# A hybrid mixer layer on one core: the RWKV mixer in three parts, squares on ScalarE, operands placed anew

## The chip, the cores and the metric

The kernel runs on one core of one Trainium2 chip. A core has a matrix engine (TensorE, PE below; its weight loads are listed apart as PEld), a vector engine (VectorE, DVE), a scalar engine (ScalarE, ACT), a general engine (GpSimd, POOL), queues that issue DMAs (SyncE, SP), an on-chip memory with 128 partitions (SBUF) and accumulator banks (PSUM). The metric is device time in microseconds of one execution. Before the change its median was 1709.05 us over three runs (1708.21 to 1712.27).

## The reference

One layer over x of 256 tokens by 2048 features, all in float32. Cut to what is computed:

```
h = rms_norm(x, norm_mix_pre)
z = h @ w_in                          # 2048 x 14800: parts of four mixers and four gates of 2048
o_conv = short_conv_mixer(z_conv)     # gated causal convolution over 3 tokens
o_gla  = gla_mixer(z_gla)             # gated linear attention, chunks of 64 tokens
o_diff = diff_attention_mixer(z_diff) # two softmax maps, their difference
o_rwkv = rwkv7_mixer(z_rwkv)          # state += (state . -kk) b + v k, token by token
merged = sum over n of sigmoid(z_gate[n]) * (o_n @ w_branch[n])
x = x + rms_norm(merged @ w_out, norm_mix_post)
h = rms_norm(x, norm_ffn_pre)
out = x + rms_norm((silu(h @ w_gate) * (h @ w_up)) @ w_down, norm_ffn_post)
```

## The kernel before

Every product of float32 matrices is made of three products of float32r: an operand is split into a rounded part "hi" and the exact remainder "lo", and hi·hi, hi·lo and lo·hi are summed in PSUM. Weights stream from DRAM in chunks of 256 rows by 512 columns (`Stream.chunk`, from L574): SP loads `raw`, ACT casts it to `hi` (L585), DVE subtracts to get `lo` (L586). `raw` has four buffers, `hi` and `lo` three each, and the chunk's instructions have a raised priority, so that the scheduler puts them ahead of other work of their engine.

There are two kinds of products with the normalised input, which lies feature-major as `hT_hi` and `hT_lo`. `gemm_feat` (L666 to L668) gives features by tokens: the weight slice is stationary and 256 tokens move through. `gemm_tok` (L646 to L648) gives tokens by features: a slice of hT (or of a mixer's output oT, of the merged mT, of h2) is stationary and 512 weight columns move through. The down projection has the same form in L1024 to L1026, with the activations `ah` and `al` stationary. The first projection (called L: 464 columns, tiles of 112, 96, 128 and 128) runs while x is still being loaded; `x_piece` makes hT_hi on ACT (L351) and hT_lo on DVE (L352) piece by piece. `x_norm` sums the squares of x (L705, L707, L709, all on POOL) for the factor of each token, which is multiplied in behind the products; its `pow` is L715.

Then come three projections rk, rr and rv, the RWKV mixer, three projections c1, c2 and c0 of the convolution, the convolution's four gate projections of 96 matmuls each with 24 matmuls of w_branch behind each (`gates_and_branch`: the sigmoid on ACT, the product with it on DVE in L764), then gqk, two gv projections and gated linear attention, the RWKV mixer's gates, differential attention, the remaining gates, w_out, and the feed-forward part.

PE takes instructions in the order in which the scheduler put them. It places the mixer's instructions among the projections that follow it by priority: `e.mix` (100000) for the mixer, `e.boost` (200000) for the weight chunks, 2·e.boost for the steps of the mixer's four chunks. The mixer's last stretch before those steps inverts 32 triangular 64 x 64 blocks. POOL inverts their 32 x 32 halves in 31 steps (L244, L246). DVE copies a transposed half (L248), POOL writes it and the halves to DRAM and reads them back (L251 to L263), and PE joins the halves by two products (L268, L272), each drained by DVE (L269, L273). After the chunk steps the outputs are transposed (L330), scaled by DVE (L338), passed twice through POOL (L340, L341) and split by ACT (L342) and DVE (L343). All the mixer's tiles are in a pool R, which is closed before the convolution is written down; the pool S1 of gated linear attention takes the same room later. PSUM has four banks "mm" for the projections, two "ps" and two "psl".

Where the operands lie, in bytes within a partition: hi at 36000 + 4096·b, lo at 48288 + 4096·b, hT_hi at 60576, hT_lo at 76960, all at 160 modulo 512. oT and mT lie at 480, ah and al at 224 modulo 512. The slices that L takes as stationary begin at 160, 96, 480 and 480.

Of the kernel before, what the change touches and what calls it, by code (L numbers as in the profile page):

```python
# [75 lines left out]
def rwkv_mixer(e, Zr, Zk, Zv, Zl, wa, g2, out_hi, out_lo):  # L76
    """Z*: [128, 4, 257] feature-major projections with a zero column in front."""
# [18 lines left out]
    # token shift  # L96
# [15 lines left out]
    # decay, in-context rate, gate  # L112
# [19 lines left out]
    C = m4("C")  # L132
# [11 lines left out]
    # normalised key direction  # L144
# [22 lines left out]
    # k' = k (1 + (a - 1) k_a)  # L167
# [7 lines left out]
    # bonus  # L175
# [8 lines left out]
    # scaled operands, [b | k] and [a | r] side by side within a chunk  # L184
# [12 lines left out]
    # value, token-major, under the rows of sa  # L197
# [14 lines left out]
    # intra-chunk products, transposed: rows [b s | k s], columns [a t | r t]  # L212
# [17 lines left out]
    # N = (I - U)^-1 of the 32 strictly upper 64 x 64 blocks U = AM[b rows, a columns]  # L230
# [17 lines left out]
    V.tensor_copy(NT[0:32], NN[0:32].rearrange("p a b -> p b a"))  # L248
# [9 lines left out]
    for hf in range(2):  # L258
        ms = slice(16 * hf, 16 * hf + 16)
# [4 lines left out]
        Zt = m4("Zt", (32, 16, 32))  # L264
        ps = e.ps()
# [8 lines left out]
    # chunks  # L274
# [4 lines left out]
    for c in range(4):  # L279
# [8 lines left out]
        X = e.M.tile([128, 8, 64], F32, tag="X", name="X", bufs=2)  # rows of sa; of the output  # L288
# [23 lines left out]
        # group norm per head  # L312
# [79 lines left out]
def gla_mixer(e, q, k, wl, v, g, wa2, out_hi, out_lo):  # L392
    """q (scaled), k: [128, 2, 256] feature-major; wl: [16, 256]; v, g: [128, 2, 512] token-major."""
# [15 lines left out]
    # log(1 + x) = 2 atanh(x / (2 + x))  # L409
# [13 lines left out]
    # scores, transposed [s, t]: within a tile of 128 [hh, i, j], and from tile 0 to tile 1 [hh, j]  # L423
# [3 lines left out]
    # the diagonal: q . k of each token and head  # L427
# [12 lines left out]
    # pairs whose halves of a block of 2w differ, scaled about the middle of the block  # L440
# [59 lines left out]
def diff_mixer(e, q, k, v, lq, out_hi, out_lo):  # L500
    """q (scaled), k: [128 (map, d), 4 heads, 256] feature-major; v: [128, 2, 512]; lq: [128, 4, 64]."""
# [3 lines left out]
    lp = e.T_.tile([128, 2, 64], F32, tag="lp", name="lp")  # L505
# [45 lines left out]
def conv_mixer(e, cu, b, rB, y, out_hi, out_lo):  # L551
    """cu: [128, 4, 258] (C * u behind two zero columns), b: two banks [128, 2, 256], rB [128, 256] their factor; y: [128, 4, 256] scratch."""
# [15 lines left out]
# blocks of 512 columns of w_in as chunks() of it holds them  # L568
# [3 lines left out]
class Stream:  # L572
    """Weights in: DMA -> (rounded part, exact remainder), both float32r."""
# [16 lines left out]
def hybrid_kernel(tc, x, xt, w_l, w_in, w_branch, w_out, w_gate, w_up, w_down, post_mix, post_ffn, wa2_d, w2_d, a2_d, g2_d, lq_d,  # L590
# [9 lines left out]
    with ExitStack() as ctx:  # L600
# [25 lines left out]
        def rms(ssum, n, eps):  # L626
            """ssum [128, 1] <- (ssum / n + eps) ** -0.5"""
# [509 lines left out]
```

## Time and profile before

| | |
|---|---|
| median of three runs | 1709.05 us |
| the profiled execution: span | 1707.7 us |
| mean granted clock of PE | 0.990 |
| busy: PE | 1665.4 us (98%), 8630 matmuls |
| busy: DVE | 987.1 us (58%) |
| busy: ACT | 753.0 us (44%) |
| busy: POOL | 190.0 us (11%) |
| DMA | 306.84 MB, mean 180 GB/s |

PE is busy nearly all the time. The chain of work that ended last is a chain of matmuls whose largest steps are L646 to L648 (9% of the span each). In a row of the timeline the number in brackets is how long the engine had been idle before the instruction, and what released it. Matmuls overlap: their recorded duration is longer than the distance from one start to the next, and it is the distance that adds up to the span. The granted clock is given as a share of full speed, 2.4 GHz; 0.50 is 1.2 GHz.

### The profile page before, as it was taken

Reading aid. Unit: us, or ns where it says so; the run is one execution under the profiler, and the core shown is the slowest. Engines: PE = TensorE matmul, PEld = TensorE weight load, DVE = VectorE, ACT = ScalarE, POOL = GpSimd, SP = SyncE. Lnnn points to the kernel's source line nnn. Section 1 sums busy time; section 2 is a strip of 40 time slices with the busy share of each in tenths; the row PEclk is TensorE's granted clock in tenths of the full one; section 3 lists DMA queues with packets and bytes.
Section 4 is the critical chain, followed back from the end, with each engine's and each line's share of the span. In section 5 each row is a group of like instructions: output and inputs, shape, how many; then the busy total and the mean of one; then the engine's idle time right before and its main releaser. Section 6 shows DMA issues by size and latency. Waiting matters only on the chain. (4 is left out here: it accounts for less than half of the span.)

```text
span 1707.7 us, 21846 instructions
## 1 busy us (share of the span) xinstructions
PE 1665.4 (98%) x8630; PEld 1402.6 (82%) x8630; DVE 987.1 (58%) x1040; ACT 753.0 (44%) x873; POOL 190.0 (11%) x168
## 2 busy tenths in 40 slices
PE   7999998999999999999999899999999999999997
PEld 6999976897788987888888788888888888888886
DVE  7667644669764458545554655445455554556555
ACT  3444342335544335544444644444444444445443
POOL 4005192111210001201000100000000000000001
PEclk8999998999999999999999999999999999999999
DMA  6654445445446554765555466565565555555653
GB/s 210 201 182 136 146 161 153 141 136 185 148 149 196 186 174 161 257 196 186 185 185 185 150 209 193 187 188 193 187 197 187 190 191 186 184 190 184 194 186 134
DMA packets 86087, 306.84 MB, mean 180 GB/s; under 512 B 9713, under 2 KB 12033, under 8 KB 85473
## 3 DMA queue, kind: packets, MB, share of 16 engines
q1 hardware_dynamic: 84208, 298.50, 54.4%
q0 software_dynamic: 1200, 5.90, 1.1%
q8 instruction: 67, 1.10, 0.3%
q10 hardware_dynamic: 576, 1.05, 0.2%
q14 instruction: 36, 0.29, 0.0%
HBM read 302.40 MB, written 3.01 MB: 179 GB/s over the span
## 5 line engine op out<-in xcount | busy, mean ns | idle before, releaser
L586 DVE TENSOR_TENSOR lo<-raw,hi 128x1024 fp32r<-128x1024 f32 (+1 forms) x556 | 699.2, 1259 | 597.3 <-ACT hi L585 596.6
L585 ACT CAST hi<-raw 128x1024 fp32r<-128x1024 f32 (+1 forms) x556 | 583.4, 1050 | 759.6 <-PE mm L648 532.4
L647 PE MATMUL mm<-lo,h_hi 128*128 128x512 f32 x704 | 275.0, 391 | 0.4 <-DVE lo L586 0.4
L648 PE MATMUL mm<-hi,h_lo 128*128 128x512 f32 x704 | 274.0, 390 | 0.0
L647 PE MATMUL mm<-lo,hT_hi 128*128 128x512 f32 x608 | 240.9, 396 | 13.3 <-DVE lo L586 13.2
L646 PE MATMUL mm<-hi,h_hi 128*128 128x512 f32 x704 | 250.2, 391 | 0.5 <-ACT h_hi L351 0.5
L648 PE MATMUL mm<-hi,hT_lo 128*128 128x512 f32 x608 | 238.9, 393 | 0.0
L646 PE MATMUL mm<-hi,hT_hi 128*128 128x512 f32 x608 | 221.7, 393 | 0.0
L668 PE MATMUL mm<-hT_hi,lo 128*128 128x256 f32 (+2 forms) x640 | 183.1, 289 | 10.3 <-DVE lo L586 10.3
L666 PE MATMUL mm<-hT_hi,hi 128*128 128x256 f32 (+1 forms) x640 | 185.2, 290 | 1.8 <-ACT hi L585 1.8
L667 PE MATMUL mm<-hT_lo,hi 128*128 128x256 f32 (+1 forms) x640 | 184.2, 289 | 0.0
L647 PEld LDWEIGHTS mm<-lo,h_hi 128*128 128x128 f32 x704 | 132.2, 188 | 28.0 <-DVE lo L586 0.9
L646 PEld LDWEIGHTS mm<-hi,h_hi 128*128 128x128 f32 x704 | 132.2, 188 | 27.8 <-ACT h_hi L351 0.7
L648 PEld LDWEIGHTS mm<-hi,h_lo 128*128 128x128 f32 x704 | 132.2, 188 | 27.0
L647 PEld LDWEIGHTS mm<-lo,hT_hi 128*128 128x128 f32 x608 | 114.8, 189 | 40.0 <-DVE lo L586 15.4
L646 PEld LDWEIGHTS mm<-hi,hT_hi 128*128 128x128 f32 x608 | 114.7, 189 | 24.4
L648 PEld LDWEIGHTS mm<-hi,hT_lo 128*128 128x128 f32 x608 | 114.8, 189 | 23.7 <-issue 0.3
L668 PEld LDWEIGHTS mm<-hT_hi,lo 128*128 128x128 f32 (+2 forms) x640 | 123.8, 194 | 11.5 <-DVE lo L586 11.2
L666 PEld LDWEIGHTS mm<-hT_hi,hi 128*128 128x128 f32 (+1 forms) x640 | 124.5, 194 | 3.2 <-ACT hi L585 2.2
L667 PEld LDWEIGHTS mm<-hT_lo,hi 128*128 128x128 f32 (+1 forms) x640 | 124.3, 194 | 1.1 <-issue 0.2
L629 POOL TENSOR_TENSOR s1f<-s1f,mhalf 128x1 f32<-128x1 f32 x2 | 1.1, 540 | 721.1 <-DVE s1f L628 721.1
L767 POOL TENSOR_TENSOR acc<-acc,gt 128x512 f32<-128x512 f32 x24 | 41.5, 1748 | 332.2 <-DVE gt L766 332.2
(351 smaller groups left out, 1892.5 us busy)
## 6 DMA issues: line engine op xcount, KB each, us to landing
raw<-in_w_in_dram SPq DMA_DIRECT2D x224, 512.0 KB, 3.5
raw<-in_w_gate_dram SPq DMA_DIRECT2D x88, 512.0 KB, 3.5
raw<-in_w_up_dram SPq DMA_DIRECT2D x88, 512.0 KB, 3.5
raw<-in_w_down_dram SPq DMA_DIRECT2D x88, 512.0 KB, 3.5
raw<-in_w_branch_dram SPq DMA_DIRECT2D x32, 512.0 KB, 3.5
raw<-in_w_out_dram SPq DMA_DIRECT2D x32, 512.0 KB, 3.5
raw<-in_w_l_dram SPq DMA_DIRECT2D x8, 464.0 KB, 5.8
xs<-in_x_dram POOLq DMA_DIRECT2D x1, 2048.0 KB, 12.9
```

The source lines that it names most:

```text
L585: nc.scalar.copy(hi[:, :, :w], raw[:, :, :w])
L586: nc.vector.tensor_tensor(lo[:, :, :w], raw[:, :, :w], hi[:, :, :w].bitcast(F32), op=ALU.subtract)
L629: G.tensor_tensor(ssum, ssum, e.mhalf.to_broadcast(list(ssum.shape)), op=ALU.pow)
L646: mm(banks[i_], ah[:, ts], hi[:, k, :], start=kt == 0, stop=False)
L647: mm(banks[i_], ah[:, ts], lo[:, k, :], start=False, stop=False)
L648: mm(banks[i_], al[:, ts], hi[:, k, :], start=False, stop=kt == nk - 1)
L666: mm(ps, hi[:, k, cs], hT_hi[:, kt, :], start=first, stop=False, skip_group_check=True)
L667: mm(ps, hi[:, k, cs], hT_lo[:, kt, :], start=False, stop=False, skip_group_check=True)
L668: mm(ps, lo[:, k, cs], hT_hi[:, kt, :], start=False, stop=last, skip_group_check=True)
L767: G.tensor_tensor(cs, cs, gt[:, i], op=ALU.add)
```

## The change

There are three edits, and each moves other things.

1. `x_norm`: the four squares go from POOL to ACT, the five additions from POOL to DVE.
2. `rwkv_mixer` is a generator in three parts. The first ends with the DMAs of the inverse; its copy L248 is POOL's now (L249 after the change). The second, the products that join the halves, is issued from the convolution's `gates_and_branch`, behind the sigmoid of the third gate (g = 2), and uses the two PSUM banks which that gate has just left. The third, the chunk steps, follows at once. The convolution and its gates are written inside the block in which R is open. All else of this part is code moved by one level of indentation.
3. Placement: tiles of hi and lo are 128 x 1152 (4608 bytes apart), of which `gemm_tok` and the down projection use the first 1024 columns and `gemm_feat` those from 64 bytes on (`SKEW`). oT has a pool of its own in front (PO), mT_hi begins 48 columns into its tile, two small tiles (hsq, lp) move to the mixers' pools, two others (ssqf, s1f) are allocated later. After it hi lies at 36000 + 4608·b, lo at 49824 + 4608·b, hT_hi at 63648, hT_lo at 80032. Stationary oT, mT, ah and al lie at 160 modulo 512. The slices which `gemm_feat` takes as stationary lie at 224, and for L at 224, 160, 32 and 32.

Comments and docstrings are removed as well. The diff, cut to its core:

```
+SKEW = 64
...
     NT = tmp
-    V.tensor_copy(NT[0:32], NN[0:32].rearrange("p a b -> p b a"))
+    G.tensor_copy(NT[0:32], NN[0:32].rearrange("p a b -> p b a"))
...
         nc.gpsimd.dma_start(N[32:64, :, 32:64], nd[32 + 16 * hf:48 + 16 * hf].rearrange("m s t -> s m t"))
-        Zt = m4("Zt", (32, 16, 32))
-        ps = e.ps()
+
+    bk = yield
+    for hf in range(2):
+        N = N2t[hf]
+        Zt = e.M.tile([32, 16, 32], F32, tag=("MP", "Oq")[hf], name="Zt", bufs=1)
+        ps = bk[hf]
         for mm in range(16):
...
         V.tensor_copy(N[0:32, :, 32:64], ps[0:32].rearrange("p (m x) -> p m x", m=16))
-    # chunks
+    yield
+
     hp = e.tc.high_priority(offset=2 * e.boost)
...
-    def chunk(self, ap, w=512, into=None):
+    def chunk(self, ap, w=512, into=None, skew=0):
...
-            hi, lo = into or [self.ring.tile([128, 2, 512], F32R, tag=t, name=t, bufs=e.nhi) for t in ("hi", "lo")]
+            if into:
+                hi, lo = into
+            else:
+                o = skew // 4
+                hi, lo = (self.ring.tile([128, 1152], F32R, tag=t, name=t, bufs=e.nhi)[:, o:o + 1024].rearrange("p (k n) -> p k n", k=2)
+                          for t in ("hi", "lo"))
...
-                hi, lo = stream.chunk(src(kc), w)
+                hi, lo = stream.chunk(src(kc), w, skew=SKEW)
...
-                    G.tensor_tensor(t, xT[:, 4 * q:4 * q + 4], xT[:, 4 * q:4 * q + 4], op=ALU.mult)
+                    S.activation(t, xT[:, 4 * q:4 * q + 4], AF.Square)
                     if q:
-                        G.tensor_tensor(sq[0], sq[0], t, op=ALU.add)
+                        V.tensor_tensor(sq[0], sq[0], t, op=ALU.add)
                 for n in (2, 1):
-                    G.tensor_tensor(sq[0][:, 0:n], sq[0][:, 0:n], sq[0][:, n:2 * n], op=ALU.add)
+                    V.tensor_tensor(sq[0][:, 0:n], sq[0][:, 0:n], sq[0][:, n:2 * n], op=ALU.add)
...
+            PO = mctx.enter_context(tc.tile_pool(name="PO", bufs=1))
...
-                return [PB.tile([128, 4, 256], F32R, tag=tag, name="oT", bufs=2) for _ in range(2)]
+                return [PO.tile([128, 4, 256], F32R, tag=tag, name="oT", bufs=2) for _ in range(2)]
...
-            def gates_and_branch(n, oT, first, done=None):
+            def gates_and_branch(n, oT, first, done=None, between=None):
...
                             S.activation(gt[:, i], bk[i], AF.Sigmoid, scale=rst[:, i:i + 1])
+                    if between:
+                        between(g, bk)
...
-                    rwkv_mixer(e, Z["r"], Z["k"], Z["v"], Z["l"], wa, g2, *oT_rwkv)
+                    rwkv = rwkv_mixer(e, Z["r"], Z["k"], Z["v"], Z["l"], wa, g2, *oT_rwkv)
+                    next(rwkv)
...
+                def rwkv_rest(g, bk):
+                    if g == 2:
+                        rwkv.send(bk)
+                        with tc.high_priority(offset=e.mix):
+                            next(rwkv, None)
+
+                gates_and_branch(0, oT, True, between=rwkv_rest)
...
-            mT_hi = L.tile([128, 16, 256], F32R, name="mT_hi")
+            mT_hi = L.tile([128, 4144], F32R, name="mT_hi")[:, 48:].rearrange("p (k t) -> p k t", t=256)
```

The order on POOL at the start, before: `acc` holds x, `sqx` its squares, `rst` the factor of each token.

```order
L812 MEMSET Z 128x4
L705 ISA
L705 TENSOR_TENSOR sqx<-acc 128x1024 x2
L835 MEMSET gt 128x4x2
L707 TENSOR_TENSOR sqx<-sqx 128x1024
L705 TENSOR_TENSOR sqx<-acc 128x1024
L707 TENSOR_TENSOR sqx<-sqx 128x1024
L705 TENSOR_TENSOR sqx<-acc 128x1024
L707 TENSOR_TENSOR sqx<-sqx 128x1024
L709 TENSOR_TENSOR sqx<-sqx 128x512
L709 TENSOR_TENSOR sqx<-sqx 128x256
L715 TENSOR_TENSOR rst<-rst,mhalf 128x2
```

And on DVE at the start, after, from its first hT_lo (L357) and lo (L596) on:

```order
L357 SCALAR_TENSOR_TENSOR hT_lo<-acc,vec,hT_hi 128x256 x4
L717 TENSOR_TENSOR sqx<-sqx 128x1024
L596 TENSOR_TENSOR lo<-raw,hi 128x2x464 x2
L357 SCALAR_TENSOR_TENSOR hT_lo<-acc,vec,hT_hi 128x256 x4
L717 TENSOR_TENSOR sqx<-sqx 128x1024
L357 SCALAR_TENSOR_TENSOR hT_lo<-acc,vec,hT_hi 128x256 x4
L596 TENSOR_TENSOR lo<-raw,hi 128x2x464
L840 CAST lev<-gt 128x768
L717 TENSOR_TENSOR sqx<-sqx 128x1024
L596 TENSOR_TENSOR lo<-raw,hi 128x2x464
L719 TENSOR_TENSOR sqx<-sqx 128x512
```

The additions stand between the pieces of hT_lo and the remainders; POOL's queue has none of these rows any more.

DVE in the convolution's gates, before: `oT` is the convolution's output, `acc` the gated sum, `tmp` the transposed half of the inverse.

```order
L565 TENSOR_TENSOR oT<-gt,oT 128x1024
L586 TENSOR_TENSOR lo<-raw,hi 128x1024 x9
L764 TENSOR_TENSOR acc<-gt,mm 128x512 x2
L586 TENSOR_TENSOR lo<-raw,hi 128x1024 x3
L248 COPY tmp<-NN 32x1024
L586 TENSOR_TENSOR lo<-raw,hi 128x1024 x5
L269 COPY Zt<-ps 32x512
L586 TENSOR_TENSOR lo<-raw,hi 128x1024 x2
```

The same place after, from the convolution's output to the copies behind the inverse's products:

```order
L570 TENSOR_TENSOR oT<-gt,oT 128x1024
L596 TENSOR_TENSOR lo<-raw,hi 128x1024 x9
L777 TENSOR_TENSOR acc<-gt,mm 128x512 x2
L596 TENSOR_TENSOR lo<-raw,hi 128x1024 x10
L777 TENSOR_TENSOR acc<-gt,mm 128x512 x2
L596 TENSOR_TENSOR lo<-raw,hi 128x1024 x10
L273 COPY Zt<-mm 32x512 x2
L777 TENSOR_TENSOR acc<-gt,mm 128x512 x2
L277 COPY N<-ps 32x16x32
```

The copy of `tmp` is gone from DVE, and `Zt` stands behind three gate projections and not within the second.

ACT at the end of the RWKV mixer, before: `oT` is the mixer's output, `vg` a result of a gv projection, drained from a bank mm.

```order
L324 ACTIVATE Oq<-X 64x512
L585 CAST hi<-raw 128x1024 x5
L342 CAST oT<-OF 128x1024
L585 CAST hi<-raw 128x1024 x2
L406 ACTIVATE x<-ps,vec 128x256 x2
L408 ACT_TABLE_LOAD
L408 ACTIVATE x<-x 128x512
L585 CAST hi<-raw 128x1024 x6
L869 ACTIVATE vg<-mm,rst 128x512
```

ACT there after:

```order
L329 ACTIVATE Oq<-X 64x512
L595 CAST hi<-raw 128x1024 x6
L347 CAST oT<-OF 128x1024
L890 ACTIVATE vg<-mm,rst 128x512 x2
L411 ACTIVATE x<-ps,vec 128x256 x2
L413 ACT_TABLE_LOAD
L413 ACTIVATE x<-x 128x512
L595 CAST hi<-raw 128x1024 x7
L890 ACTIVATE vg<-mm,rst 128x512
```

The two drains of the first gv projection stand directly behind the cast of the mixer's output; before, eight casts of weights and three other instructions stood between. The drain writes a tile of S1, in the room of R, and waits for the mixer's last remainder on DVE (L348), which reads R.

## Rows read from the trace of the kernel before

**Rows 1.** The page: its first line, and busy time of TensorE.
```profile
span 1707.7 us, 21846 instructions
...
PE 1665.4 (98%) x8630; PEld 1402.6 (82%) x8630; DVE 987.1 (58%) x1040; ACT 753.0 (44%) x873; POOL 190.0 (11%) x168
```

**Rows 2.** Windows: us, busy time by engine (x instructions), PEclk, DMA share, GB/s.
```profile
7.80:46.70 38.90, 29.43 (x198) 28.74 (x199) 32.51 (x31) 14.68 (x25) 18.56 (x11) 0.78 0.60 212
```

**Rows 3.** Groups by line, DVE from 7.6 to 26.8 us: xcount, busy, mean ns, idle before.
```profile
L352 DVE SCALAR_TENSOR_TENSOR hT_lo<-acc,vec,hT_hi 128x256 fp32r<-128x256 f32 x6 | 13.1, 2241 | 0.0
L586 DVE TENSOR_TENSOR lo<-raw,hi 128x928 fp32r<-128x928 f32 x3 | 7.1, 2367 | 2.4 <-ACT hi L585 2.4
```

**Rows 4.** Timeline, DVE: start us, us, line, operation, xcount, idle before and releaser.
```profile
28.70 3.24 DVE L352 SCALAR_TENSOR_TENSOR hT_lo<-acc,vec,hT_hi 128x256 fp32r<-128x256 f32 x8
31.87 1.11 DVE L586 TENSOR_TENSOR lo<-raw,hi 128x928 fp32r<-128x928 f32 x1
```

**Rows 5.** Timeline, POOL: the end of x's sum of squares.
```profile
24.58 2.18 POOL L709 TENSOR_TENSOR sqx<-sqx 128x512 f32<-128x512 f32 x2
```

**Rows 6.** Timeline, PE: the longest wait in the first projection.
```profile
27.80 0.55 PE L668 MATMUL mm<-hT_hi,lo 128*112 128x256 f32 x1 [5.52 <-DVE lo L586]
```

**Rows 7.** Windows, after the wait within the second gate projection.
```profile
263.00:268.10 5.10, 5.10 (x12) 4.04 (x13) 2.21 (x2) 0.43 (x1) 2.34 (x4) 0.50 0.85 272
```

**Rows 8.** Timeline, DVE and POOL: the copy of the inverse, the last of its DMAs.
```profile
260.79 1.02 DVE L248 COPY tmp<-NN 32x1024 f32<-32x1024 f32 x1 [14.34 <-POOL NN L246]
...
268.47 0.65 POOL L263 DMA_DIRECT2D N<-nd  x1
```

**Rows 9.** Timeline, PE: the first product after the wait.
```profile
263.00 0.79 PE L647 MATMUL mm<-lo,hT_hi 128*128 128x512 f32 x1 [10.28 <-DVE lo L586]
```

**Rows 10.** Line L646: xcount, duration ns min/median/max, first and last start us, forms.
```profile
L646 PE MATMUL mm<-hi,hT_hi x608: 387/389/628, 211.1 to 855.7; 128*128 128x512 f32 x152
...
L646 PE MATMUL mm<-hi,oT x128: 388/397/502, 232.9 to 861.3; 128*128 128x512 f32 x128
...
L646 PE MATMUL mm<-hi,mT_hi x128: 393/398/398, 862.0 to 951.8; 128*128 128x512 f32 x128
```

**Rows 11.** Timeline, PE: first and last of four runs of consecutive matmuls.
```profile
33.78 0.28 PE L666 MATMUL mm<-hT_hi,hi 128*112 128x256 f32 x1
...
34.91 0.28 PE L667 MATMUL mm<-hT_lo,hi 128*128 128x256 f32 x1
...
74.80 0.28 PE L668 MATMUL mm<-hT_hi,lo 128*128 128x256 f32 x1
...
75.88 0.28 PE L668 MATMUL mm<-hT_hi,lo 128*128 128x256 f32 x1
...
1299.62 0.39 PE L647 MATMUL mm<-lo,h_hi 128*128 128x512 f32 x1
...
1301.88 0.39 PE L648 MATMUL mm<-hi,h_lo 128*128 128x512 f32 x1
...
1499.82 0.39 PE L1024 MATMUL wd<-hi,ah 128*128 128x512 f32 x1
...
1501.69 0.39 PE L1024 MATMUL mm<-hi,ah 128*128 128x512 f32 x1
```

**Rows 12.** Timeline, PE: the last transposes of the RWKV mixer.
```profile
376.41 0.46 PE L330 MATMUL psl<-ident,X 64*128 64x64 f32 x4
```

**Rows 13.** Timeline, POOL: the mixer's last two passes.
```profile
378.91 3.19 POOL L340 TENSOR_TENSOR OF<-OF,BV 128x1024 f32<-128x1024 f32 x1 [6.25 <-DVE OF L338]
382.18 3.27 POOL L341 TENSOR_TENSOR OF<-OF,Gt 128x1024 f32<-128x1024 f32 x1
```

**Rows 14.** Timeline, ACT: the cast of the mixer's output, and the first drain of vg.
```profile
385.48 1.05 ACT L342 CAST oT<-OF 128x1024 fp32r<-128x1024 f32 x1 [2.18 <-POOL OF L341]
...
409.17 0.69 ACT L869 ACTIVATE vg<-mm,rst 128x512 f32<-128x512 f32 x1 [0.98 <-PE mm L648]
```

**Rows 15.** Timeline, DVE: the remainder of the mixer's output.
```profile
386.56 1.23 DVE L343 TENSOR_TENSOR oT<-OF,oT 128x1024 fp32r<-128x1024 f32 x1
```

More of the change, by code (lines that the diff above doesn't have):

```diff
@@ L258, in rwkv_mixer @@
     for hf in range(2):
-        ms = slice(16 * hf, 16 * hf + 16)
         N = N2t[hf]
@@ L358, in head_norm_out @@
     V, S = nc.vector, nc.scalar
-    sq = e.T_.tile([128, 512], F32, tag="hsq", name="hsq")
+    sq = e.M.tile([128, 512], F32, tag="hsq", name="hsq")
     V.tensor_scalar(sq, po, 2.0 ** 64, -(2.0 ** 64), op0=ALU.min, op1=ALU.max)
@@ L828, in hybrid_kernel @@
                 with tc.high_priority(offset=e.mix):
-                    rwkv_mixer(e, Z["r"], Z["k"], Z["v"], Z["l"], wa, g2, *oT_rwkv)
-            oT = out_pair("oA")
-            ct = gt_tile()[:, 0:1024].rearrange("p (f t) -> p f t", f=4)
-            cu = gt_tile().rearrange("p (f t) -> p f t", f=4)
-            G.memset(cu[:, :, 0:2], 0.0)
-            bk = [bank(), bank()]
-            ctiles = [(128 * j, 128) for j in range(4)]
-            gemm_feat(columns(w_in, COL["c1"]), 512, ctiles, bk)
@@ L839, in hybrid_kernel @@
-            for p in range(2):
-                V.tensor_tensor(ct[:, 2 * p:2 * p + 2], two(bk[p]), rb2(rB2), op=ALU.mult)
-            bk = [bank(), bank()]
-            gemm_feat(columns(w_in, COL["c2"]), 512, ctiles, bk)
-            for p in range(2):
-                V.tensor_tensor(cu[:, 2 * p:2 * p + 2, 2:258], ct[:, 2 * p:2 * p + 2], two(bk[p]), op=ALU.mult)
-            bk = [bank(), bank()]
-            gemm_feat(columns(w_in, COL["c0"]), 512, ctiles, bk)
-            conv_mixer(e, cu, [two(b) for b in bk], rB, ct, *oT)
@@ L848, in hybrid_kernel @@
-            gates_and_branch(0, oT, True)
+                    rwkv = rwkv_mixer(e, Z["r"], Z["k"], Z["v"], Z["l"], wa, g2, *oT_rwkv)
+                    next(rwkv)
+                oT = out_pair("oA")
+                ct = gt_tile()[:, 0:1024].rearrange("p (f t) -> p f t", f=4)
+                cu = gt_tile().rearrange("p (f t) -> p f t", f=4)
+                G.memset(cu[:, :, 0:2], 0.0)
+                bk = [bank(), bank()]
+                ctiles = [(128 * j, 128) for j in range(4)]
+                gemm_feat(columns(w_in, COL["c1"]), 512, ctiles, bk)
@@ new lines, in hybrid_kernel @@
+                for p in range(2):
+                    V.tensor_tensor(ct[:, 2 * p:2 * p + 2], two(bk[p]), rb2(rB2), op=ALU.mult)
+                bk = [bank(), bank()]
+                gemm_feat(columns(w_in, COL["c2"]), 512, ctiles, bk)
+                for p in range(2):
+                    V.tensor_tensor(cu[:, 2 * p:2 * p + 2, 2:258], ct[:, 2 * p:2 * p + 2], two(bk[p]), op=ALU.mult)
+                bk = [bank(), bank()]
+                gemm_feat(columns(w_in, COL["c0"]), 512, ctiles, bk)
@@ L851, in hybrid_kernel @@
+                conv_mixer(e, cu, [two(b) for b in bk], rB, ct, *oT)
+                def rwkv_rest(g, bk):
[4 more added lines that the diff above has]
+                gates_and_branch(0, oT, True, between=rwkv_rest)
             with ExitStack() as sctx:
@@ L854, in hybrid_kernel @@
                 e.ps2 = lambda: p2.tile([128, 2, 512], F32, tag="ps2", name="ps2", bufs=1)
-                e.M = TagPool(P, {"m4": 5, "m2": 13})
+                e.M = TagPool(P, {"m4": 5, "m2": 13, "hsq": 1})
                 oT = out_pair("oA")
@@ L879, in hybrid_kernel @@
                 e.ps2 = lambda: p2.tile([128, 2, 512], F32, tag="ps2", name="ps2", bufs=1)
-                e.M = TagPool(P, {"m4": 6, "m8": 1})
+                e.M = TagPool(P, {"m4": 6, "m8": 1, "hsq": 1, "lp": 1})
                 oT = out_pair("oR")
@@ L1004, in hybrid_kernel @@
             sq = F.tile([128, 512], F32, name="sqf", bufs=2)
-            ssq = F.tile([128, 2, 4], F32, name="ssqf")
-            s1 = F.tile([128, 2], F32, name="s1f")
             for hf in range(2):
@@ L1047, in hybrid_kernel @@
                                 products(kc, al_[kc], ch_[kc, j], j, i)
+                if hf == 0:
+                    ssq = F.tile([128, 2, 4], F32, name="ssqf")
+                    s1 = F.tile([128, 2], F32, name="s1f")
                 for i in range(2):
```

2 lines of the change are left out of this document (1 added, 1 removed).

## The prediction

> **What bounds the kernel now.** I read the busy times first: TensorE (PE) works 1665.4 us of a span of 1707.7 us [rows 1]. So the end moves only if PE's 42.3 us of idle shrink or if its matmuls follow each other faster; work of the other engines counts only where PE waits for it. Next I looked at where PE is idle or slowly clocked. Two places stand out. From 7.8 to 46.7 us (the first projection, "L") PE is busy 29.43 of 38.90 us at a granted clock of 0.78 [rows 2]. At 263.00 us it has just waited 10.28 us [rows 9], and it then runs 5.1 us at clock 0.50 [rows 7]. Everywhere else PE is packed, so the third view is the time from one matmul's start to the next, which differs between groups of equal shape [rows 11].
>
> The profiled execution spans 1707.7 us, 1.35 us under the median of 1709.05. I sum against the span and add 1.3 us at the end.
>
> **A. Startup: the squares of x leave GpSimd (POOL).** POOL squares and adds until 26.8 us [rows 5]. In that time VectorE (DVE) makes six hT_lo and three lo: 13.1 us at 2241 ns and 7.1 us at 2367 ns [rows 3]. As soon as POOL stops, eight hT_lo take 3.24 us (405 ns each) and a lo takes 1.11 us [rows 4]. The excess on DVE is 13.1 − 6×0.405 = 10.7 us, and 7.1 − 3×1.11 = 3.8 us of which the last lo, begun beside the end of POOL's work, carries little: about 14 us. PE meets it as waits for lo, the longest 5.52 us [rows 6], and as the half clock that follows them. In the changed kernel the four squares run on ScalarE (ACT), which is busy for only 14.68 of the 38.90 us [rows 2], and the five adds on DVE, priced by a lo: 3×1.2 + 0.7 + 0.4 = 4.7 us, most of them after hT_lo. Also, lam leaves its place in this stretch. L has 192 matmuls; at 0.113 us [rows 11] they take 21.8 us, so from 7.8 us on they could end at 29.6. DVE's own work up to there is 8×1.11 + 16×0.405 + 4.7 = 20.1 us, about the same. Granting 3.5 us for half clock and for weights that come late, L ends at 33.2 instead of 46.7: −13.5 us, bounds −10 (half of the excess is given back to DVE's adds) and −16.
>
> [...]
>
> **B. The inverse.** POOL builds the 32 inverses until 260.8 us, and DVE's copy L248 stands in DVE's queue ahead of the lo that the second gate projection wants. It has kept DVE idle for 14.34 us until POOL is done [rows 8], and PE waits 10.28 us for the first lo behind it [rows 9]. The next 12 matmuls take 5.1 us at half clock where 12×0.227 would take 2.7: 2.4 us more [rows 7]. Together 12.7. In the changed kernel the copy is POOL's, so no lo is queued behind it, and the products stand behind the third gate projection of the convolution. Their inputs were on the way at 269.1 us, the end of the last DMA's issue [rows 8]; with L 13.5 us earlier and three projections before them 192×0.0067 us shorter each (D), that becomes about 252, or 254 with a copy that takes 1.9 to 3.3 us on POOL, as its other passes of 1024 columns do [rows 13], and not 1.02. The gates began at 211.1 us [rows 10] and will begin at about 190 (A, and six projections of D). PE has 3×96 + 2×24 + 20 wide products to do before the inverse's: 356×0.2265 = 81 us, so it comes to them at 271, some 17 us after they are ready. DVE has a few small copies more between lo there. I take −12.5, bounds −9 and −12.7.
>
> **C. Stationary operands oT, mT and ah/al move to the phase of the others.** From start to start a 512-wide matmul takes (1301.88 − 1299.62)/10 = 0.2265 us with h and hi, both at 160 modulo 512, and (1501.69 − 1499.82)/8 = 0.2335 us with ah/al, which stand at 224 [rows 11]. oT and mT stand at 480; the median durations are 397 and 398 ns against 389 for hT [rows 10]. Shape, type and engine are equal, so the placement is the only difference that I find. 3×128 products with oT, 3×128 with mT and 3×336 with ah/al change: 1776 × 0.0066 = −11.7 us. Bounds: 0, if the cause is another, and 1776×0.009 = −16 by the durations.
>
> **D. The feature projections get their weights 64 bytes further.** Nine of them with 192 matmuls of 256 columns, at 160/160 now, take (75.88 − 74.80)/9 = 0.120 us each; those of L, whose slices start at 160, 96 and 480, take (34.91 − 33.78)/10 = 0.113 us [rows 11]. In the change all stationary slices stand at 224, and a 224 slice at 256 columns is not in the trace. At 512 columns the offsets +64 and +320 cost alike, and at 256 columns +320 is in L and is fast, so I take 0.113: 1728 × 0.0067 = −11.5 us. Bounds: 0 (stays 0.120) and +11.5, if 64 bytes cost here what they cost in the down projection.
>
> [...]
>
> **E. A new wait.** The chunks of the RWKV mixer now come later, beside gqk and the first gv. Their tail is: PE's last transposes to 376.87, four OF on DVE, two POOL passes to 385.45, the cast to 386.53 and oT_lo to 387.79 [rows 12 to 15], so 10.9 us. vg lies in the room that the mixer's pool leaves, so vg's drain on ACT waits for that oT_lo; it takes 0.69 us [rows 14]. The second gv projection begins in the bank which that drain empties. Between the last transposes and this matmul the order now has 30 wide products, 6.8 us; before there were 68 feature and 96 wide ones, some 30 us. PE waits 10.9 + 0.7 − 6.8 = 4.8 us. Queued behind the drain on ACT are a table load and the seven hi of the next chunks, so PE may starve a little longer. With half clock as in B (2.4) and about 1.3 us of crowding on DVE, where gqk's lo and the chunk steps now meet, I take +8.5; bounds +3 (three passes run faster where DVE is free) and +14.
>
> The rest (ring tiles 4608 bytes apart, hsq, lp and ssq in other pools, the mT pad) adds no instruction, so 0; the case where the spacing matters is a rival.
>
> **Sum.** 1707.7 − 13.5 − 12.5 − 11.7 − 11.5 + 8.5 = 1667.0; with 1.3 us around the span, **1668 us**.
>
> **The rivals.**
> 1. The 64 bytes do nothing: D = 0, 1680 us. For it: no row has 224 at 256 columns. Against: L's slices are fast at three different offsets. Chance 0.16.
> 2. The 64 bytes cost: D = +11.5, 1691 us. For it: 224 is slow in the down projection, and there too the two addresses are 64 bytes apart. Against: at 256 columns it is the unequal offsets that are fast. 0.06.
> 3. Placement does nothing: C = D = 0, 1691 us. For it: only different stages are compared, with different neighbours. Against: the groups are narrow, oT from 388 to a median of 397 and mT from 393 to 398 beside 387 to 389 [rows 10]. 0.04.
> 4. The new wait is far larger: vg's drain holds all of ACT's queue, so the lo and hi of several chunks are late and PE runs at half clock over the second gv, 96 matmuls more at 0.43 instead of 0.227, +19.5 instead of +2.4: 1685 us. 0.05.
> 5. The other side: what counts is not the phase modulo 512 but modulo the old distance of 4096. Now hi, lo, hT_hi and hT_lo are all at 3232 modulo 4096; with 4608 between ring tiles they drift apart by 512. Then the 3936 wide products of the gates and of gate/up go from 0.2265 to 0.2335 (+27.5), C gains nothing, D costs or gives nothing: 1707.7 − 26.0 + 8.5 + 27.5 + 1.3 = 1719 us, to 1730 with D at +11.5. It decides from about 2500 products upward, where the 17.5 us of A, B and E are eaten up. Against it: slices of hT already run through all multiples of 512 at one duration (minimum 387, median 389) [rows 10]. 0.03.
>
> **How the numbers follow.** The forecast has 0.66, of which its own range is 1660 to 1677 (A, B and E at their bounds). The rivals to 1691 take 0.31 and the slower case 0.03. The range that should hold 8 in 10 goes from 1655 (A, B, E at their good ends, and a little of C's) to 1688, which takes in rival 1 with its own spread and half of rivals 2 to 4. A measurement of this kernel can tell about 0.3%, 5 us, from no change. Faster by more: all but rival 5 and 0.01 of mishaps, 0.96; within: 0.01; slower: 0.03.
>
> **What would show it.** A: L's last matmul at about 33 us, DVE's hT_lo at 0.41 and lo at 1.11 us throughout. B: no PE gap above 4 us between 190 and 280 us, and no copy L248 on DVE. C: products with oT, mT and ah/al with a duration of 389 ns, starts 0.2265 us apart. D: feature products 0.113 us apart; at 0.120 rival 1, at 0.127 rival 2. E: a PE gap of about 5 us before the first product of the second gv, ended by the vg drain on ACT; no gap would make E +0, a half clock over the whole of gv rival 4. Gates at 0.2335 us would be rival 5. The prediction as a whole is wrong if the time lies above 1690 us or below 1650.

## The result and the profile after

The changed kernel takes 1673.12 us (median of four runs, 1672.94 to 1674.19) against 1709.24 for the kernel before on the same chip: ratio 0.9783, 95% interval 0.9770 to 0.9797. The forecast was 1668, the range 1655 to 1688. The profiled execution spans 1671.4 us, 36.3 less than before.

First the page of the changed kernel, as [rows 1]:

```profile
span 1671.4 us, 21849 instructions
...
PE 1644.8 (98%) x8630; PEld 1395.1 (83%) x8630; DVE 980.5 (59%) x1044; ACT 760.1 (45%) x879; POOL 185.7 (11%) x160
```

PE's busy time fell by 20.6 us and its idle time by 15.7. To see where, I read the start of the first product of a stage in both timelines, us:

| the first product of | before | after | ahead by |
|---|---|---|---|
| the first projection, L | 7.83 | 7.60 | 0.2 |
| rk | 46.50 | 33.20 | 13.3 |
| the convolution's first gate | 211.09 | 194.74 | 16.4 |
| its second gate | 238.47 | 221.97 | 16.5 |
| the RWKV mixer's first gate | 434.13 | 406.18 | 28.0 |
| the branch product of its third gate | 527.24 | 501.65 | 25.6 |
| w_out | 861.99 | 833.96 | 28.0 |
| the feed-forward part | 956.17 | 925.61 | 30.6 |
| the down projection | 1450.41 | 1420.99 | 29.4 |
| the end | 1707.7 | 1671.4 | 36.3 |

**A.** The first projection, in the window from its first product to its end, and VectorE's groups there (columns as in [rows 2] and [rows 3]):

```profile
7.80:33.50 25.70, 25.01 (x199) 24.60 (x199) 21.82 (x34) 17.95 (x28) 0.84 (x4) 0.93 0.92 332
```

```profile
L596 DVE TENSOR_TENSOR lo<-raw,hi 128x928 fp32r<-128x928 f32 x8 | 8.9, 1117 | 3.0 <-ACT hi L595 3.0
L357 DVE SCALAR_TENSOR_TENSOR hT_lo<-acc,vec,hT_hi 128x256 fp32r<-128x256 f32 x14 | 5.9, 476 | 0.0
L717 DVE TENSOR_TENSOR sqx<-sqx 128x1024 f32<-128x1024 f32 x3 | 3.7, 1218 | 0.3 <-ACT sqx L715 0.3
```

PE is busy 25.01 of 25.70 us where it was 29.43 of 38.90. lo takes 1117 ns instead of 2367, and VectorE had time for the additions: it finished 14 hT_lo and eight lo where [rows 3] has six and three.

**B and E.** POOL's copy and the last DMA of the inverse, and PE's first products with it:

```profile
252.16 2.10 POOL L249 COPY tmp<-NN 32x1024 f32<-32x1024 f32 x1
...
261.58 0.65 POOL L263 DMA_DIRECT2D N<-nd  x1
```

```profile
275.56 2.21 PE L272 MATMUL mm<-T,AM 32*32 32x32 f32 x64
```

No bracket stands behind the last row: PE did not wait. Then the new wait, on PE, ACT and DVE, and the clock behind it:

```profile
381.82 0.79 PE L656 MATMUL mm<-hi,hT_hi 128*128 128x512 f32 x1 [5.37 <-ACT vg L890]
```

```profile
381.08 1.27 ACT L890 ACTIVATE vg<-mm,rst 128x512 f32<-128x512 f32 x2 [2.31 <-DVE oT L348]
```

```profile
379.83 1.21 DVE L348 TENSOR_TENSOR oT<-OF,oT 128x1024 fp32r<-128x1024 f32 x1
```

```profile
381.82:386.00 4.18, 4.18 (x10) 3.31 (x11) 2.23 (x5) 3.27 (x5) 1.28 (x1) 0.50 0.40 122
```

This is the chain that the prediction worked out: PE waits for the drain, the drain for the mixer's last remainder. The clock is at 1.2 GHz behind it as it was behind the old wait in [rows 7].

**C and D.** Durations of the wide products (as [rows 10]), starts of the down projection (ten intervals) and of rr in the changed kernel (thirteen):

```profile
L656 PE MATMUL mm<-hi,hT_hi x608: 387/389/794, 194.7 to 827.8; 128*128 128x512 f32 x152
...
L656 PE MATMUL mm<-hi,oT x128: 387/389/497, 216.5 to 833.3; 128*128 128x512 f32 x128
...
L656 PE MATMUL mm<-hi,mT_hi x128: 389/389/393, 834.0 to 921.2; 128*128 128x512 f32 x128
```

```profile
1499.63 0.39 PE L1044 MATMUL mm<-lo,ah 128*128 128x512 f32 x1
...
1501.89 0.39 PE L1044 MATMUL wd<-lo,ah 128*128 128x512 f32 x1
```

```profile
59.77 0.28 PE L676 MATMUL mm<-hT_hi,hi 128*128 128x256 f32 x1
...
61.30 0.28 PE L677 MATMUL mm<-hT_lo,hi 128*128 128x256 f32 x1
```

All wide products have 389 ns now, and the down projection goes at 2.26/10 = 0.226 us where [rows 11] gave 0.2335. The feature products go at 1.53/13 = 0.1177, neither the 0.113 of the forecast nor the 0.120 of before.

### The profile page after: what moved, and what is told of

Read it like the earlier page. It is cut to its first block, busy times and chain, and to the rows that moved or that the text cites. A ratio compares the mean times of both kernels' runs of the same rounds, so it can differ in the third digit from the quotient of the medians.

```text
span 1671.4 us, 21849 instructions
## 1 busy us (share of the span) xinstructions
PE 1644.8 (98%) x8630; PEld 1395.1 (83%) x8630; DVE 980.5 (59%) x1044; ACT 760.1 (45%) x879; POOL 185.7 (11%) x160
## 4 chain that ended last, share of the span: by engine, by line
PE 94%; DVE 3%; issue 1%; ACT 1%; DMA 0%; POOL 0%; SPq 0%; DVEq 0%; ACTq 0%; POOLq 0%
PE mm L657 21%; PE mm L656 21%; PE mm L658 21%; PE mm L678 4%; PE mm L677 4%; PE mm L676 4%; PE mm L1043 2%; PE mm L1044 2%; PE mm L1045 2%; PE wd L1044 2%; PE wd L1045 2%; PE wd L1043 2%; DVE lo L596 1%; PE tq L1021 1%; PE ps L221 1%
## 5 line engine op out<-in xcount | busy, mean ns | idle before, releaser
L596 DVE TENSOR_TENSOR lo<-raw,hi 128x1024 fp32r<-128x1024 f32 (+1 forms) x556 | 699.6, 1259 | 593.3 <-ACT hi L595 592.6
L676 PE MATMUL mm<-hT_hi,hi 128*128 128x256 f32 (+1 forms) x640 | 181.2, 284 | 1.8 <-ACT hi L595 1.8
L678 PE MATMUL mm<-hT_hi,lo 128*128 128x256 f32 (+2 forms) x640 | 179.5, 283 | 2.2 <-DVE lo L596 2.2
L677 PE MATMUL mm<-hT_lo,hi 128*128 128x256 f32 (+1 forms) x640 | 180.8, 283 | 0.0
L676 PEld LDWEIGHTS mm<-hT_hi,hi 128*128 128x128 f32 (+1 forms) x640 | 120.1, 188 | 3.1 <-ACT hi L595 2.2
L677 PEld LDWEIGHTS mm<-hT_lo,hi 128*128 128x128 f32 (+1 forms) x640 | 120.7, 189 | 1.1 <-issue 0.2
## 6 DMA issues: line engine op xcount, KB each, us to landing
xs<-in_x_dram POOLq DMA_DIRECT2D x1, 2048.0 KB, 11.5
```

The lines of the kernel that those rows point to most:

```text
L596: nc.vector.tensor_tensor(lo[:, :, :w], raw[:, :, :w], hi[:, :, :w].bitcast(F32), op=ALU.subtract)
L676: mm(ps, hi[:, k, cs], hT_hi[:, kt, :], start=first, stop=False, skip_group_check=True)
L677: mm(ps, hi[:, k, cs], hT_lo[:, kt, :], start=False, stop=False, skip_group_check=True)
L678: mm(ps, lo[:, k, cs], hT_hi[:, kt, :], start=False, stop=last, skip_group_check=True)
```

## The experiments

Each time is a median, each ratio one against the kernel before on the same chip, with its 95% interval. All edits are against the changed kernel unless said.

**1. Distances, one per projection.**

```
+            skew = next(FSK)
...
-                hi, lo = stream.chunk(src(kc), w, skew=SKEW)
+                hi, lo = stream.chunk(src(kc), w, skew=skew)
...
-                    gemm_tok(columns(w_up, g), lhs2, 16, bu)
+                    gemm_tok(columns(w_up, g), lhs2, 16, bu, skew=next(TSK))
```

> The changed kernel, but each feature projection has its own distance between its stationary weights and its moving hT (in the order of the program 64, 0, 32, 128, 192, 256, 320, 384, 448, 480 bytes), and each of the 22 projections of the feed-forward part its own distance between its moving weights and its stationary h2 (0, 0, 16, 32, 64, 96, 128, 160, 192, 224, 256, 288, 320, 352, 384, 416, 448, 480, 512, 4, 8, 0). Theory 1, only equal phases modulo 512 are special: feature products 0.120 us apart at 0 and 0.113 to 0.118 at every other distance; wide products 0.2265 us at 0 and 512 and 0.2335 at every other one. Theory 2, the distance matters by steps (a half of the 512 bytes, a quarter): several levels, with the fastest feature distance near 256 to 448 and a wide distance that beats 0.2265. Theory 3, placement does nothing and the stages differ for other reasons: all feature products 0.1177, all wide ones 0.2265. The time by theory 1: 17 wide projections of 96 products at +0.007 are +11.4 us and the features -2 us, about 1683 us.

1684.2 us, one execution. The wide products, by distance (address of the moving operand less that of the stationary one; mean from start to start in the chunks that have no other products between them, ns): 0: 226.6 to 227.1; 256 and 512: 227.3; 64 and 320: 229.1; 16: 231.8; 384: 232.4; 8, 32, 192, 224, 288, 448, 480: 232.9 to 233.3; 96, 128, 352: 233.5 to 233.7; 160 and 416: 234.2; 4: 238.0. Two stretches of fourteen intervals from the trace, at 128 and at 256:

```profile
1079.63 0.39 PE L657 MATMUL mm<-hi,h_hi 128*128 128x512 f32 x1
...
1082.90 0.39 PE L659 MATMUL mm<-hi,h_lo 128*128 128x512 f32 x1
...
1169.69 0.39 PE L658 MATMUL mm<-lo,h_hi 128*128 128x512 f32 x1
...
1172.86 0.39 PE L657 MATMUL mm<-hi,h_hi 128*128 128x512 f32 x1
```

3.27/14 = 0.2336 and 3.17/14 = 0.2264. So theory 1 with half its period: what counts is the distance modulo 256 (pairs 256 apart agree to 0.7 ns, but for 128 and 384 with 1.3), and every value but 0 costs. It also gives the levels before the change: there the stationary operand lay 64 and 320 bytes above the moving one, which is 192 modulo 256 in the sense of this run, and 192 and 448 are at 0.2331 and 0.2333 here. Of the features, whose distance is counted from the moving to the stationary operand, in chunks without other products between them: 0.1200 at 0 and at 256, 0.1183 at 32, 0.1187 at 128, 0.1178 at 448, 0.1167 at 480. Here too 256 is like 0. At 192 (c1) the first and the last chunk go at 0.1177 and products between them at 0.1133.

**2. The 64 bytes alone undone** (`SKEW = 0`).

> The changed kernel without the 64 bytes: the feature projections' weights lie at 160 modulo 512 again, all else as changed. By the trace after, nine projections of 192 products go from 0.1177 back to 0.120 us: +3.9 us, 1677 us. By the prediction's step as it was sized (0.113 against 0.120) it would be +11.5 us, 1684.6; if the 64 bytes do nothing, 1673.

1677.57 us, ratio 0.9804 (0.9790 to 0.9819) against 0.9783 after the change. The two intervals overlap, so the times alone do not tell; the trace does: rk, rr, rv, c1, c0, dq0 and dq1 take 24.09, 23.04, 23.04, 30.79, 35.40, 23.03 and 23.04 us, to 0.01 us what they took before. (c2 takes 28.2 in all three traces.) The 64 bytes bring 4 us, a third of what D was sized at.

**3. The kernel before with the squares on ScalarE** (the three lines of x_norm, nothing else).

> The kernel before with the squares of x on ScalarE and their additions on VectorE, nothing else. Theory: all of the 13.3 us by which the first projection ends earlier come from this, so 1709 - 13.3 = 1696 us, and VectorE's subtractions there take 1.1 us instead of 2.4. Rival: the small steps for lam, which still stand in ScalarE's and VectorE's queues there, hold part of it: 3 to 6 us less is won, 1699 to 1702, with ScalarE idle until VectorE has made lam.

1699.19 us, ratio 0.9933 (0.9918 to 0.9948): 11.5 us. L takes 25.25 us instead of 38.67, so the whole of A comes from the squares, and lam, still in its place, costs nothing: the time lies in the rival's range, but not for the rival's reason. In the traced execution, the longest of the four (1701.79 us, the others 1696.71 to 1699.52), part of the gain was lost again: the second gate and its branch, with the inverse, took 4.1 us more than before. The stretch begins with the same wait as [rows 9]; then PE waits 1.67 us for the products' input, where it had waited 0.67, and a second stretch at half clock follows, which the kernel before has not:

```profile
249.78 0.79 PE L647 MATMUL mm<-lo,hT_hi 128*128 128x512 f32 x1 [10.28 <-DVE lo L586]
...
261.50 1.61 PE L268 MATMUL ps<-T,AM 32*32 32x32 f32 x32 [1.67 <-DMA T<-td]
```

```profile
262.00:268.30 6.30, 6.30 (x34) 5.10 (x32) 1.90 (x2) 1.62 (x2) 0.00 (x0) 0.50 0.20 77
```

By the median 1.8 of the 13.3 us are missing, which is within the spread of these four times.

**4. The kernel before with the copy on POOL** (`V.tensor_copy` to `G.tensor_copy` in L248, nothing else).

> The kernel before with the transposing copy of the inverse on GpSimd, nothing else; the products that join the halves stay where the scheduler puts them, which is now 12 wide products further on. Theory: the wait goes from the lo to these products, which are reached at about 263 us and whose inputs arrive at about 273: TensorE waits about 10 us there, 12 wide products are done earlier (2.7 us), so 1706 to 1709 us. Rival: the queue behind the copy was the whole cost, and the wait goes: 1709 - 12.7 = 1696 us.

1712.01 us, ratio 1.0006 (0.9996 to 1.0016): nothing. The lo came in time, and PE waited for the products instead:

```profile
276.38 1.91 PE L268 MATMUL ps<-T,AM 32*32 32x32 f32 x32 [13.23 <-DMA T<-td]
```

**5. 320 bytes and its neighbours** (as 1: L at 0, then 320, 288, 352, 320, 320, 320, 320, 304, 336).

> The changed kernel with other distances for the feature projections, in program order 0 (L), 320, 288, 352, 320, 320, 320, 320, 304, 336 bytes; the wide ones as changed. Theory 1: the full-width slices of L, which stood at 480 before the change, were fast because of their place, 320 bytes from hT: rk at 320 takes 0.113 to 0.114 us a product and 21.8 us in all (23.4 after the change, 24.1 before), L 24.9. Theory 2: they were fast because L's other slices are narrower than 128 columns: rk stays at 0.1175 and 23.4 us.

1673.2 us, one execution. L takes 24.90 us. rk takes 23.36, and chunk by chunk its products go at 0.1133 in the second and third and at 0.1178 from the fifth on. That is, to a tenth of a nanosecond, what they do at 64. Neither theory (the 23.4 us of theory 2 came out, but half of rk is fast at full width): 320 is a twin of 64, as a period of 256 would have it, and each has two paces. 288, 304, 336 and 352 give 0.1183 to 0.1188.

**6. q, k and vg outside the mixer's room.**

```
-                q = e.M.tile([128, 2, 256], F32, tag="m2", name="q")
-                k = e.M.tile([128, 2, 256], F32, tag="m2", name="k")
+                q, k = gt_tile()[:, 0:1024].rearrange("p (n j t) -> n p j t", n=2, j=2)
...
-                    t = e.M.tile([128, 2, 512], F32, tag="m4", name="vg")
+                    t = gt_tile()[:, 0:1024].rearrange("p (i n) -> p i n", i=2) if c == 0 else e.M.tile([128, 2, 512], F32, tag="m4", name="vg")
```

> The changed kernel, with q, k and the first vg of gated linear attention in two of the three gt tiles, which lie outside the room that the RWKV mixer's pool leaves; no other edit. Theory (the new wait E): the 5.4 us for which TensorE waits for vg's drain at 376 us and the half clock behind it (11 products at 0.43 us, 2.2 us) go: 1673.1 - 7.5 = 1665.6 us. Rival: the wait only changes its name (the drain stays behind the cast of the mixer's output on ScalarE, or the next gates wait for the one gt tile that is left): 1671 to 1676 us.

1669.63 us, ratio 0.9752 (0.9738 to 0.9767). The wait is gone (the first gv takes 25.39 us instead of 30.93), and up to the first branch of the RWKV mixer's gates 12.5 us are won, 4.9 of them in the gate before it, from which 32 small products of gated linear attention, and a wait of 0.9 us for one of them, have only moved behind it. The branch, the second and the third gate then give 9.8 back. PE waits for lo again, and the window shows VectorE busy for 16.91 of 20 us, more than PE:

```profile
437.83 0.50 PE L657 MATMUL mm<-lo,hT_hi 128*128 128x512 f32 x1 [1.86 <-DVE lo L596]
```

```profile
420.00:440.00 20.00, 16.08 (x74) 12.00 (x73) 16.91 (x19) 14.33 (x18) 6.86 (x5) 0.96 0.30 93
```

**7. The copy on VectorE again, the products still late** (`G.tensor_copy` to `V.tensor_copy`).

> The changed kernel with the inverse's transposing copy on VectorE again, its products as late as changed. VectorE's queue then has the copy after the third lo of the second gate projection, and ten more lo wait behind it. Theory (queue): TensorE runs out of lo at about 236 us and waits until GpSimd is done at about 250: 14 to 17 us and 2.4 of half clock, about 1690 us. Rival: it is the late place of the products that took the wait away: 1673 us.

1685.65 us, ratio 0.9844 (0.9827 to 0.9860) against 0.9783. The second gate takes 35.11 us instead of 21.76:

```profile
246.97 0.80 PE L657 MATMUL mm<-lo,hT_hi 128*128 128x512 f32 x1 [10.67 <-DVE lo L596]
```

With run 4: either half of the edit alone leaves PE 10 to 13 us without work, only both take the wait away. The wait was shorter than the 14 to 17 us expected, since POOL was done at 244.7 us and not at 250.

**8. Dead work on POOL at the start.**

```
+                    G.tensor_tensor(dead, xT[:, 4 * q:4 * q + 4], xT[:, 4 * q:4 * q + 4], op=ALU.mult)
+                    if q:
+                        G.tensor_tensor(dead, dead, dead, op=ALU.add)
```

> The changed kernel with seven operations more on GpSimd in the first 25 us, squares of x and additions as the kernel before had them, into a tile that nobody reads; squares and additions for the result stay on ScalarE and VectorE. Theory (contention): hT_lo takes 1.6 to 2.3 us instead of 0.41 and lo 2.4 instead of 1.1 while they run, L ends 8 to 12 us later, 1681 to 1686 us. Rival: what the change removed was a dependence or a place in a queue: nothing waits for the dead operations, so 1673 us.

1684.76 us, ratio 0.9836 (0.9822 to 0.9851). L takes 37.16 us instead of 25.60. VectorE's groups from 7.6 to 26.8 us:

```profile
L357 DVE SCALAR_TENSOR_TENSOR hT_lo<-acc,vec,hT_hi 128x256 fp32r<-128x256 f32 x6 | 10.7, 1837 | 0.0
L596 DVE TENSOR_TENSOR lo<-raw,hi 128x928 fp32r<-128x928 f32 x4 | 7.6, 1923 | 2.7 <-ACT hi L595 2.7
```

Nobody waits for this work, so it slows VectorE by running beside it. And one thing that neither theory had: here rr and rv went at the fast pace (thirteen intervals of rr, 1.47 us, 0.1131), with the addresses of the changed kernel:

```profile
71.83 0.28 PE L678 MATMUL mm<-hT_hi,lo 128*128 128x256 f32 x1
...
73.30 0.28 PE L676 MATMUL mm<-hT_hi,hi 128*128 128x256 f32 x1
```

**9. The second gv in the banks of the mixer's transposes** (`w2 = e.ps2(); bk = [w2[:, 0], w2[:, 1]]` for it).

> The changed kernel, with the second gv projection in the two PSUM banks that the RWKV mixer's transposes have left (free from about 372 us) instead of the banks which q, k and vg are drained from; no other edit. Theory (E is a wait for a bank, not for ScalarE as such): TensorE goes on at 376 us, the 5.4 us of wait and 2.2 us of half clock go, and no gt tile is taken from the gates: 1673.1 - 7.5 = 1665.6 us. Rival: the drain holds ScalarE's queue until 381 us, so that the casts of weights behind it are late and TensorE waits for hi instead: 1670 us or more.

1672.01 us, ratio 0.9774 (0.9760 to 0.9787), not to be told from the changed kernel. The wait of 5.37 us is gone here too (first gv 25.39 us), but the branch and the gates two and three of the RWKV mixer give back 10.2 of the 11.3 us won before them. ScalarE's queue, the rival, was not the cause: in the second gv PE waits once, and for a lo of VectorE.

```profile
391.68 0.50 PE L657 MATMUL ps<-lo,hT_hi 128*128 128x512 f32 x1 [1.30 <-DVE lo L596]
```

**10. Small products between the features.**

```
+            n = next(poke)          # 2, 64, 128, 2 columns ahead of rr, rv, dq0, dq1
+            if n:
+                ps = e.ps()
+                mm(ps[:, 0:n], ident, ident[:, 0:n], start=True, stop=True)
```

> The changed kernel with one extra small product (128 by 2, 64, 128 and 2 columns, result unused) ahead of the projections rr, rv, dq0 and dq1, whose products followed each other every 0.1178 us after the change and every 0.1133 us (rr, rv) with the dead work on GpSimd, at equal addresses. Theory: with 64 bytes between them there are two steady paces, 0.1133 and 0.1178, and it is an interruption that sets which one holds until the next: at least one of the four goes at 0.1133 throughout (21.8 us a projection instead of 22.6). Rival: the pace hangs on the time or on other engines' work: all four stay at 0.1178. The time: 1670 to 1674 us.

1671.67 us, one execution. rr and rv go at 0.1133 throughout, dq0 and dq1 at 0.1178, so the theory's sign came out, but not by its cause. rk was at 0.1133 already: in this build four small products of the mixer, which stood inside rk after the change, stand at the start of rv, and rk keeps its first pace to the end. The extra product of 2 columns between rk and rr, and those at the start of rv, changed nothing. And dq0 and dq1 were not tested: the scheduler put their extra products 38 us ahead of dq0, among wide products:

```profile
494.96 0.50 PE L670 MATMUL ps<-ident 128*128 128x128 f32 x4
...
533.08 0.28 PE L682 MATMUL mm<-hT_hi,hi 128*128 128x256 f32 x1
```

So a pace holds as long as nothing comes between. In these traces it changed only at such small products (the four inside rk, from 0.1133 to 0.1177 after the change and from 0.1178 to 0.1133 in run 8), but not at all of them. Which of them changes it, and to what, stays open.

**11. Run 9, and L without its 64 bytes.**

> As the run with the second gv projection in the other banks, and the first projection without its 64 bytes, so that its full-width slices lie at 480 again as before the change. Its products go from 0.1185 to 0.1135 us where it isn't waiting: 0.7 us less, 1664.9 us if the other edit brings 7.5; nothing for the first projection if x and its weights come no sooner.

1671.69 us, ratio 0.9773 (0.9760 to 0.9787). L took 25.58 us against 25.60: it waits for x and its weights, so a faster pace there buys nothing.

**12. Run 6, and eight steps of gated linear attention on ScalarE.**

```
-                V.tensor_scalar(scd[:, hh, i, j], e.ident, dg[:, i, j, hh:hh + 1], None, op0=ALU.mult)
+                S.activation(scd[:, hh, i, j], e.ident, AF.Copy, scale=dg[:, i, j, hh:hh + 1])
```

> The run with q, k and the first vg in gt tiles, and in addition the eight diagonal products of gated linear attention (128 by 128, 4.9 us in all on VectorE between 416 and 421 us there) on ScalarE. Theory: what gave back most of the wait E is VectorE, 90% busy from 381 to 440 us, with the lo that TensorE wants queued behind the steps of gated linear attention; 4.9 us less on it lets the gates beside it end 2 to 5 us earlier: 1665 to 1668 us against 1669.6, and TensorE's busy share from 420 to 440 us rises over 80%. Rival: ScalarE's steps set the end there (it waits for table loads and has the casts of hi): 1669.6 or more.

1666.48 us, ratio 0.9741 (0.9725 to 0.9757), clear of the changed kernel's interval and the fastest version here. The same window:

```profile
420.00:440.00 20.00, 18.67 (x96) 14.22 (x95) 16.94 (x16) 16.18 (x21) 9.38 (x6) 1.00 0.33 106
```

PE is busy 18.67 us of the 20 instead of 16.08, and the clock stays full. But in the next 20 us it is busy 18.12 instead of 20.00, and waits for a lo again:

```profile
440.00:460.00 20.00, 18.12 (x95) 14.39 (x95) 15.20 (x13) 6.20 (x7) 2.58 (x2) 1.00 0.59 182
```

```profile
444.93 0.50 PE L657 MATMUL mm<-lo,hT_hi 128*128 128x512 f32 x1 [1.88 <-DVE lo L596]
```

The third branch of the RWKV mixer's gates starts at 495.96 instead of 498.96 us; 0.8 of these 3.0 are products that have moved behind it, and the fourth gate starts 2.2 us earlier. So VectorE's work there gave back part of the wait, at least 2.2 us of it. What gave back the rest no run shows by itself.

## Why the prediction was right, point by point

**A**, −13.5 forecast, −13.3 measured (rk starts 13.3 us earlier). Run 3 shows that the squares alone do it, run 8 that it is POOL's work beside VectorE's, not a dependence. That the size came out to 0.2 us is in part luck: 3.5 us of it were an allowance, and L's products went at 0.117 to 0.118 and not at the 0.113 of the sum, 0.8 us in all.

**B and E**, −12.5 and +8.5, together −4.0 forecast. From the second gate to the third branch of the RWKV mixer's gates the kernel gains 25.6 − 16.5 = 9.1 us, of which 0.8 is C (five branch products at 0.16) and 0.4 D: −7.9 measured. The mechanism was right in both, and runs 4 and 7 show why the edit needs both halves. B brought 13.3 us: the 10.28 and 2.4 of the forecast, and 0.67 us for which PE had waited for the products' input. Its margin was smaller than forecast: the last DMA was issued by 262.2 us and not by 254, because the gates began at 194.7 and not at 190 and POOL's steps took 57.7 us instead of 50.2 (see the last section), and PE came at 275.6. The size of E is the term that was off. The wait itself was as forecast (4.8 us forecast, 5.37 measured; 2.4 of half clock forecast, 2.3 measured, since the second gv took 24.37 us and 22.04 in run 6). But the crowding on VectorE, +1.3 forecast, went the other way. Before the change PE waited twice more for lo in this stretch; after it one wait of 0.87 us is left:

```profile
399.08 0.50 PE L647 MATMUL mm<-lo,hT_hi 128*128 128x512 f32 x1 [1.22 <-DVE lo L586]
...
448.58 0.50 PE L647 MATMUL mm<-lo,hT_hi 128*128 128x512 f32 x1 [1.18 <-DVE lo L586]
```

```profile
431.33 1.68 PE L460 MATMUL ps<-qe,ke 64*128 64x128 f32 x16 [0.87 <-DVE scd L462]
```

So E cost 5.37 + 2.3 − 1.5 = 6.2 us and not 8.5; with B that is −7.1, and 0.8 of the −7.9 stays unplaced. Nor is the wait worth its length: taking it away brought, in the traces, 1 us (run 9) or 3.5 (run 6, where q and k also come earlier), not 7.5. In these two runs VectorE is busy for 54.0 and 53.5 of the 59 us from 381 to 440, PE waits for its lo, and taking 4.9 us of work off it (run 12) gives 2.2 back. That VectorE gets ahead while PE waits, so that the wait hides the crowding, fits this but is argued. Rival 4 did not come: half clock holds for one stretch of 4.18 us in the trace above, not over the gv projection.

**C**, −11.7 forecast, −12.0 measured: 6.9 in the down projection (3.5 and 3.4 us in its halves), 2.5 in w_out, 2.6 in the sixteen branches of 0.16 us. The 0.3 us more are the last 48 products of the down projection, which the count left out (3×336 for 3×352). Run 1 shows that the distance of the two operands sets the rate, with a period of 256 bytes and not of 512, which makes no difference for this change. That rules out the third rival, and the fifth: gates and gate/up kept 0.2265 with tiles 4608 bytes apart.

**D**, −11.5 forecast, −4.3 measured (run 2: about 4). This is the step that failed in size: "at 256 columns +320 is in L and is fast, so I take 0.113". That 64 behaves like 320 was right (run 5; in run 1, too, distances 256 apart are alike). That 320 means 0.113 was not: it means one of two paces, 0.1133 or 0.1178, and the ten intervals of L in [rows 11] had shown only the faster. Most projections ran at the slower, and runs 5, 8 and 10 show the other one at equal addresses. And L was no clean row to read it from: two of its four slices lie elsewhere, at 160 and 96, and the one at 160, 112 columns wide and at distance 0, goes at 0.114 too (33.78 us in [rows 11] and the two products behind it), where full width goes at 0.1200. So the row could not show that the distance made L fast; whether it is the width or the change of slices stays open.

The sum: −13.3 − 7.9 − 12.0 − 4.3 = −37.5, and 1.2 us that the feed-forward part's first projections took more (49.77 to 51.01 us): the granted clock is 0.56 from 925.6 to 933.3 us, where it was 1.00 before. Runs 3 and 4, which change nothing there, have the same +1.2 and +0.8, and the others lie between 49.4 and 51.1, so this is not put down to the change. The two errors, 7.2 us too much for D and 3.9 too little for B and E, cancelled in part. That the total was only 5 us off is luck to that extent.

## What to carry to other kernels

When a wait of the busiest engine comes or goes, look at which engine will be nearly full in the stretch behind it (here the next 60 us), and price the wait by that, not by its length. A queue in order turns one late operand into a stall of everything behind it; here moving the copy alone, or its reader alone, brought nothing, and only both did. Where products of equal shape run at different rates, compare where their two operands lie modulo 256 bytes, and test the pace over whole stages and more than one build before a rate is taken as a property of an address.

## What the runs showed of the hardware that was not expected

At 256 columns, with the stationary operand 64 or 320 bytes above the moving one, TensorE has two steady paces, 0.1133 and 0.1178 us a product, at equal addresses (run 1 has both at 192 as well); a change came only where other products interrupted. At a distance of 0 or 256 and a stationary slice of full width it is 0.1200 in every uninterrupted chunk, the slowest, while for 512 columns the same distances are the best (0.2265 to 0.2273 against 0.229 to 0.238), and four bytes are already the worst.

The slowing between VectorE and POOL goes both ways. POOL's 62 steps of the inverse (L244 and L246 before) took 50.2 us, from 210.5 to 260.8, where VectorE stood still for 14 us of it; in run 7, with VectorE held in the same way, 49.9; but 57.7 after the change and 55.6 in run 4, where VectorE went on with its lo. Step by step, run 4 against before, 55 of the 62 take the same to 0.02 us, one 0.1 less, and six take 0.87 to 0.97 more. Here is one of these, before, with VectorE still, and in run 4, where a lo ran from 248.34 to 249.90:

```profile
248.49 0.69 POOL L246 TENSOR_TENSOR NN<-NN,tmp 64x240 f32<-64x240 f32 x1
```

```profile
248.89 1.56 POOL L246 TENSOR_TENSOR NN<-NN,tmp 64x240 f32<-64x240 f32 x1
```
